# Hybrid decoder step on one core: rotary products taken from PSUM, inverse roots and gates by exp and ln on ScalarE

## The chip, the cores and the metric

One core of a Trainium2 chip runs the whole program. The metric is device microseconds (us) of one execution; three runs of the kernel before are shown. About 0.5% (16 us) is what a measurement of this kernel can tell from no change.

## What is computed

One inference step of a two-layer decoder for a prompt of 2048 tokens and 8 sample tokens, all in float32. Layer 0 is the one that the change touches:

```
u, q, k, v, gate = split_cols(h @ w_in, ...)          # h = rmsnorm(x)
q = rope(rmsnorm(q.reshape(B, L, 12, 64), qn_w), pos)
k = rope(rmsnorm(k.reshape(B, L, 12, 64), kn_w), pos)
rmsnorm(x, w) = x * rsqrt(mean(x * x) + EPS) * w
rope(x, pos)  = concat(x1 * cos - x2 * sin, x2 * cos + x1 * sin)
mixed = concat(a_out, b_out) * silu(gate)
x = x + mixed @ w_out
```

The sample tokens attend to a paged cache of 128 pages of keys and 128 of values. Layer 1 (gated DeltaNet and a spatial-gating MLP) follows with the same in- and out-projections.

## The kernel before

The program has four stages: the in-projection of layer 0 (`in_even`), prompt attention, the out-projection of layer 0 (`out_even`) and the whole of layer 1 (`odd`). Every float32 product is made of three fp32r matmuls with high and low halves (`mm3`, L167 to L169). A scheduler orders each engine's instructions when the program is built; each engine then works through its own queue in that order, and a waiting instruction holds all that stand behind it.

`in_even` treats the prompt in two halves of 1024 tokens. For each half it normalizes the tokens (`h_tile`), and then goes through a written list of jobs (`JOBS`): q, k and v in column blocks of 256, eight gate blocks, and the pooling branch. One q or k block (`qkv_block`) of 256 tokens by 256 columns is 48 matmuls into one PSUM bank (`acc`; five banks serve all the blocks and gates of this stage). Then `qk_norm_rope` runs over the block: ScalarE squares it out of the bank (`qsq`, L245), VectorE sums over 64 columns (`qss`, L247), GpSimd adds EPS and raises to the power -0.5 (`rstd`, L106 and L107), VectorE multiplies the bank by that factor (`qxn`, L250), GpSimd makes the products with the cosine and sine tables (L254 and twice L258), and VectorE adds them (`qr`, L261). The bank is free after L250. TensorE transposes `qr` (L362), ScalarE and VectorE split it into halves (`qhi`, `qlo`), and four stores to DRAM follow. There are 48 such blocks for the prompt and 6 small ones for the sample tokens.

Between the blocks, `sample_scores` walks the 128 key pages of the cache: a 384 KB load by SyncE (three buffers `kp`), a product on GpSimd or, for one page in three, on VectorE (L521), and a sum on VectorE (L522). It begins when the q blocks of the first half are issued. The weights come as units (`w_unit`): ScalarE makes the high half (`whi`), GpSimd the low half (`wlo`, L148).

A gate (`silu2_store`, L391 and L393) is one tanh on ScalarE and one multiply on VectorE out of the bank. `rstd` also serves `h_tile`, the end of each attention quad (`ss`), and layer 1.

Of the kernel before, what the change touches and what calls it, by code (L numbers as in the profile page):

```python
# [10 lines left out]
F32 = mybir.dt.float32  # L11
# [50 lines left out]
class Net:  # L62
# [28 lines left out]
    def constants(self):  # L91
        nc, I, c = self.nc, self.I, self.const
        self.ident = c.tile([P, P], F32, name="ident")
        make_identity(nc, self.ident)
        self.identb = c.tile([P, P], BF16, name="identb")
        make_identity(nc, self.identb)
        self.ones = c.tile([P, P], F32, name="ones")
        nc.gpsimd.memset(self.ones, 1.0)
        self.mhalf = c.tile([P, 1], F32, name="mhalf")
        nc.gpsimd.memset(self.mhalf, -0.5)  # L100

    def rstd(self, ms, eps=EPS):

        g = self.nc.gpsimd
        if eps:
            g.tensor_scalar(ms, ms, eps, None, ALU.add)  # L106
        g.tensor_tensor(ms, ms, self.mhalf[:ms.shape[0]].broadcast_to(list(ms.shape)), ALU.pow)  # L107
# [131 lines left out]
    def qk_norm_rope(self, pool, ps, C, S, np_, nt, ng):  # L239

        nc = self.nc
        n = nt * ng
        sq = pool.tile([P, n, 64], F32, tag="qsq", name="qsq")[:np_]
        flat = ps.rearrange("p t (g d) -> p (t g) d", d=64)
# [3 lines left out]
        self.rstd(ss)  # L248
        xn = pool.tile([P, n, 64], F32, tag="qxn", name="qxn")[:np_]
        nc.vector.tensor_tensor(xn, flat, ss[:, :, None].broadcast_to([np_, n, 64]), ALU.mult)  # L250
        a = sq
        x4 = xn.rearrange("p (t g) d -> p t g d", t=nt)
        a4 = a.rearrange("p (t g) d -> p t g d", t=nt)
        nc.gpsimd.tensor_tensor(a4, x4, C[:, :, None, :].broadcast_to([np_, nt, ng, 64]), ALU.mult)  # L254
        b = pool.tile([P, n, 64], F32, tag="qb", name="qb")[:np_]
        b4 = b.rearrange("p (t g) d -> p t g d", t=nt)
        for o in (0, 32):
            nc.gpsimd.tensor_tensor(b4[:, :, :, o:o + 32], x4[:, :, :, 32 - o:64 - o],  # L258
                                    S[:, :, None, o:o + 32].broadcast_to([np_, nt, ng, 32]), ALU.mult)
        r = pool.tile([P, n, 64], F32, tag="qr", name="qr", bufs=3)[:np_]  # L260
        nc.vector.tensor_tensor(r, a, b, ALU.add)  # L261
# [124 lines left out]
    def silu2_store(self, pool, ps, dst, r0, t0, n, ns):  # L386
# [4 lines left out]
        nc.scalar.activation(th[:, :w], ps[:, :w], AF.Tanh, scale=0.5)  # L391
        sg = th
        nc.vector.scalar_tensor_tensor(sg[:, :w], th[:, :w], 1.0, ps[:, :w], ALU.add, ALU.mult)  # L393
# [484 lines left out]
    def out_even(self):  # L878
# [18 lines left out]
        for n, t in enumerate(P3):  # L897
            t0 = t * P
# [833 lines left out]
```

## Time and profile before

| | |
|---|---|
| median of three runs | 3227.11 us (3221.92 to 3235.94) |
| the profiled execution | 3230.68 us |
| its span in the trace | 3229.0 us, 57271 instructions |
| mean granted clock of TensorE | 0.946 |
| HBM traffic | 332.41 MB read, 126.33 MB written, 142 GB/s over the span |

The span is the time between the first and the last instruction in the trace; 1.7 us of the execution lie around it. PE is TensorE, PEld its weight loads, DVE VectorE, ACT ScalarE, POOL GpSimd, SP SyncE. [...]

### The profile page before, as it was taken

What the parts mean: (1) busy time and instruction counts of PE and PEld (TensorE: products, weight loads), DVE (VectorE), ACT (ScalarE), POOL (GpSimd) and SP (SyncE); (2) the same over time, 40 slices, a digit from 0 to 9 for tenths busy, and PEclk for the clock granted to TensorE, in tenths of its full rate; (3) what the DMA queues carried; (4) which work ended last, traced back from release to release, by engine and by line L of the source; (5) the groups of instructions that cost most, each with busy time, mean ns of one, the idle gap of its engine ahead of it and who ended that gap; (6) DMA issues with size and microseconds to landing.
All of it is one profiled execution on the core that took longest, in us unless ns stands there. A gap on an engine that the chain in (4) does not pass through costs nothing. (4 is left out here: it accounts for less than half of the span.)

```text
span 3229.0 us, 57271 instructions
## 1 busy us (share of the span) xinstructions
PE 2828.4 (88%) x20425; PEld 2530.5 (78%) x20425; DVE 2221.3 (69%) x3958; ACT 1335.5 (41%) x3753; POOL 1937.4 (60%) x1532
## 2 busy tenths in 40 slices
PE   7988889997889889898988777899999988878999
PEld 7987888996777677787877667778888977767887
DVE  5565555556489989895578998667888674357652
ACT  4212121221378777773222323445555542444331
POOL 8887557996277787776576555455444335246541
PEclk9998899998999999999999889999999998979999
DMA  4455876554632444206676554435333333458542
GB/s 156 131 159 190 258 213 190 180 184 154 162 83 58 110 115 104 64 24 192 218 250 204 159 173 149 150 106 152 87 101 85 90 104 102 124 163 229 143 125 85
DMA packets 423146, 462.53 MB, mean 143 GB/s; under 512 B 84683, under 2 KB 324212, under 8 KB 422860
## 3 DMA queue, kind: packets, MB, share of 16 engines
q1 hardware_dynamic: 422860, 458.86, 47.9%
q8 instruction: 162, 2.65, 0.4%
q14 instruction: 124, 1.02, 0.1%
HBM read 332.41 MB, written 126.33 MB: 142 GB/s over the span
## 5 line engine op out<-in xcount | busy, mean ns | idle before, releaser
L167 PE MATMUL acc<-sh,whi 128*128 128x256 f32 (+2 forms) x1328 | 391.4, 295 | 12.8 <-DVE th L393 3.8
L169 PE MATMUL acc<-sh,wlo 128*128 128x256 f32 (+2 forms) x1328 | 387.3, 292 | 1.7 <-DVE wlo L148 1.3
L168 PE MATMUL acc<-sl,whi 128*128 128x256 f32 (+2 forms) x1328 | 387.8, 292 | 0.1
L167 PE MATMUL acc<-bh,whi 128*128 128x512 f32 (+2 forms) x904 | 348.6, 386 | 30.7 <-ACT raw L1183 15.0
L169 PE MATMUL acc<-bh,wlo 128*128 128x512 f32 (+2 forms) x904 | 347.9, 385 | 7.7 <-DVE wlo L148 4.2
L168 PE MATMUL acc<-bl,whi 128*128 128x512 f32 (+2 forms) x904 | 346.5, 384 | 1.8 <-DVE bl L846 1.8
L809 POOL TENSOR_TENSOR p<-p,cf 128x512 f32<-128x512 f32 (+3 forms) x240 | 239.4, 1016 | 163.7 <-ACT p L786 58.4
L786 ACT ACTIVATE p<-sc,nb 128x512 f32<-128x512 f32 (+3 forms) x480 | 300.7, 636 | 89.1 <-DVE nb L785 80.5
L599 POOL TENSOR_TENSOR kp<-kp,at 128x768 f32<-128x768 f32 x120 | 210.5, 1763 | 155.3 <-DMA kp<-in_cache_v 136.6
L785 DVE TENSOR_REDUCE nb<-sc 128x1 f32<-128x512 f32 (+3 forms) x480 | 275.8, 597 | 17.8 <-PE sc L782 8.8
L167 PE MATMUL acc<-whi,bh 128*128 128x256 f32 x864 | 253.4, 294 | 27.8 <-DVE qxn L250 24.6
L167 PEld LDWEIGHTS acc<-sh,whi 128*128 128x128 f32 (+1 forms) x1328 | 258.5, 195 | 22.9 <-ACT raw L1183 4.4
L148 POOL TENSOR_TENSOR wlo<-wraw,whi 128x1024 fp32r<-128x1024 f32 (+1 forms) x90 | 224.6, 2498 | 83.3 <-ACT whi L146 82.5
L168 PEld LDWEIGHTS acc<-sl,whi 128*128 128x128 f32 (+1 forms) x1328 | 258.9, 195 | 6.6 <-issue 2.9
L168 PE MATMUL acc<-wlo,bh 128*128 128x256 f32 x864 | 252.8, 293 | 12.0 <-POOL wlo L148 12.0
L169 PEld LDWEIGHTS acc<-sh,wlo 128*128 128x128 f32 (+1 forms) x1328 | 258.1, 194 | 5.1 <-DVE wlo L148 1.5
L169 PE MATMUL acc<-whi,bl 128*128 128x256 f32 x864 | 252.9, 294 | 0.0
L781 PE MATMUL sc<-kh,q 128*128 128x512 f32 (+2 forms) x480 | 212.4, 443 | 35.8 <-ACT p L786 34.0
L1199 DVE SCALAR_TENSOR_TENSOR cx<-raw,convw,cx 128x512 f32<-128x512 f32 x216 | 235.6, 1091 | 11.2 <-ACT cx L1197 8.7
L823 PE MATMUL pv<-v,pt 128*128 128x128 f32 x1632 | 220.1, 283 | 16.5 <-ACT pt L821 8.4
L823 PEld LDWEIGHTS pv<-v,pt 128*128 128x128 f32 x1632 | 205.9, 197 | 28.6 <-ACT pt L821 11.9
L521 POOL TENSOR_TENSOR kp<-kp,qb 128x768 f32<-128x768 f32 x88 | 170.0, 1938 | 94.9 <-DMA kp<-in_cache_k 63.9
(434 smaller groups left out, 8412.1 us busy)
## 6 DMA issues: line engine op xcount, KB each, us to landing
kp<-in_cache_k SPq DMA_DIRECT2D x128, 384.0 KB
kp<-in_cache_v SPq DMA_DIRECT2D x128, 384.0 KB
wraw<-in_w_in_e SPq DMA_DIRECT2D x56, 512.0 KB
wraw<-in_w_in_o SPq DMA_DIRECT2D x56, 512.0 KB
mc<-cat SPq DMA_DIRECT2D x72, 256.0 KB
mg<-sg SPq DMA_DIRECT2D x72, 256.0 KB
y<-cth SPq DMA_DIRECT2D x72, 256.0 KB
kh<-kh SPq DMA_DIRECT2D x48, 256.0 KB
```

What stands on the lines that cost most here:

```text
L148: e.tensor_tensor(lo, raw, hi.bitcast(F32), ALU.subtract)
L167: mm(out, ah, bh, start=first, stop=False)
L168: mm(out, ah, bl, start=False, stop=False)
L169: mm(out, al, bh, start=False, stop=last)
L521: (nc.vector if j % 3 == 2 else nc.gpsimd).tensor_tensor(k, k, qb, ALU.mult)
L599: nc.gpsimd.tensor_tensor(h3(w), h3(v), self.at[:, b, j, :, None].broadcast_to([P, NH, P]), ALU.mult)
L781: mm(sc[:, :w], qc, kh[:, c, :w], start=True, stop=False)
L785: nc.vector.tensor_reduce(nb[:, c, j:j + 1], sc[:, :n], AX.X, ALU.max, negate=True)
L786: nc.scalar.activation(p[:, c, :n], sc[:, :n], AF.Exp, bias=nb[:, c, j:j + 1], accum_out=l[:, c, j:j + 1])
L809: nc.gpsimd.tensor_tensor(p[:, 1, :n], p[:, 1, :n], cf[:, 1, j:j + 1].broadcast_to([P, n]), ALU.mult)
L823: mm(pv, tt[:, t, :], kvt[j][2][:, t, :], start=j == 0 and t == 0, stop=j * 4 + t == nk - 1)
L1199: nc.vector.scalar_tensor_tensor(x, raw[:, o + j:o + j + 512], w[:, j:j + 1], x, ALU.mult, ALU.add)
```

## The change

The rotary products are made on VectorE straight from the PSUM bank, their sum on GpSimd, and the norm's factor is applied last, by ScalarE, in eight pieces of 64 columns for each block. `rstd` becomes two ScalarE instructions, Ln and Exp, wherever `self.logs` is set and the eps is 1e-6; `self.logs` holds through layer 0 up to the eighth tile of `out_even`. The gates of layer 0 become Exp, Ln, Exp on ScalarE and a multiply on VectorE. One table set (number 6) is loaded at the start. Layer 1 keeps its instructions.

```diff
     def rstd(self, ms, eps=EPS):
+        if self.logs and eps == EPS:
+            n = ms.shape[0]
+            self.nc.scalar.activation(ms, ms, AF.Ln, bias=self.eps[:n])
+            self.nc.scalar.activation(ms, ms, AF.Exp, scale=-0.5)
+            return
...
         nc.vector.tensor_reduce(ss, sq, AX.X, ALU.add)
-        self.rstd(ss)
-        xn = pool.tile([P, n, 64], F32, tag="qxn", name="qxn")[:np_]
-        nc.vector.tensor_tensor(xn, flat, ss[:, :, None].broadcast_to([np_, n, 64]), ALU.mult)
-        a = sq
-        x4 = xn.rearrange("p (t g) d -> p t g d", t=nt)
+        a = pool.tile([P, n, 64], F32, tag="qxn", name="qxn")[:np_]
         a4 = a.rearrange("p (t g) d -> p t g d", t=nt)
-        nc.gpsimd.tensor_tensor(a4, x4, C[:, :, None, :].broadcast_to([np_, nt, ng, 64]), ALU.mult)
+        nc.vector.tensor_tensor(a4, x4, C[:, :, None, :].broadcast_to([np_, nt, ng, 64]), ALU.mult)
         b = pool.tile([P, n, 64], F32, tag="qb", name="qb")[:np_]
         b4 = b.rearrange("p (t g) d -> p t g d", t=nt)
         for o in (0, 32):
-            nc.gpsimd.tensor_tensor(b4[:, :, :, o:o + 32], x4[:, :, :, 32 - o:64 - o],
+            nc.vector.tensor_tensor(b4[:, :, :, o:o + 32], x4[:, :, :, 32 - o:64 - o],
                                     S[:, :, None, o:o + 32].broadcast_to([np_, nt, ng, 32]), ALU.mult)
+        self.rstd(ss)
         r = pool.tile([P, n, 64], F32, tag="qr", name="qr", bufs=3)[:np_]
-        nc.vector.tensor_tensor(r, a, b, ALU.add)
+        nc.gpsimd.tensor_tensor(a, a, b, ALU.add)
+        for i in range(n):
+            nc.scalar.mul(r[:, i, :], a[:, i, :], ss[:, i:i + 1])
...
-        nc.scalar.activation(th[:, :w], ps[:, :w], AF.Tanh, scale=0.5)
-        sg = th
-        nc.vector.scalar_tensor_tensor(sg[:, :w], th[:, :w], 1.0, ps[:, :w], ALU.add, ALU.mult)
+        if self.logs:
+            e = th[:, :w]
+            nc.scalar.activation(e, ps[:, :w], AF.Exp, scale=-1.0)
+            nc.scalar.activation(e, e, AF.Ln, bias=1.0)
+            nc.scalar.activation(e, e, AF.Exp, scale=-1.0, bias=self.ln2)
+            sg = th
+            nc.vector.tensor_tensor(sg[:, :w], e, ps[:, :w], ALU.mult)
...
         for n, t in enumerate(P3):
+            self.logs = n < 8
```

The scheduler lays out every queue anew. Three places matter. First, ScalarE's queue at the first k blocks of the first half; `qsq` is the square of a block, `qhi` the split of its transposed result. Before:

```order
L245 ACTIVATE qsq_1673<-acc_1611 128x512
L245 ACTIVATE qsq_1763<-acc_1701 128x512
L245 ACTIVATE qsq_1853<-acc_1791 128x512
L135 CAST qhi_1693<-tr_1688 128x512
L146 CAST whi_2012<-wraw_2014 128x1024
L146 CAST whi_2162<-wraw_2164 128x1024
L245 ACTIVATE qsq_1943<-acc_1881 128x512
```

and with the change:

```order
L263 ACTIVATE qsq_1777<-acc_1715 128x512
L118 ACTIVATE qss_1779<-qss_1779,eps_77 128x8
L119 ACTIVATE qss_1779<-qss_1779 128x8
L279 ACTIVATE qr_1788<-qxn_1781,qss_1779 128x64 x8
L263 ACTIVATE qsq_1874<-acc_1812 128x512
L118 ACTIVATE qss_1876<-qss_1876,eps_77 128x8
L119 ACTIVATE qss_1876<-qss_1876 128x8
L152 CAST qhi_1804<-tr_1799 128x512
```

The split of the first block stood behind the squares of two further blocks; it now stands behind one, and the eight multiplies of a block stand ahead of the next block's square.

Second, TensorE's queue where the same block is transposed (`tr`). Before, during the small sample matmuls that come after the fourth block on:

```order
L167 MATMUL acc_1971<-whi_1106,sh_135 8x256
L362 MATMUL tr_1688<-ident_63,qr_1685 128x128 x4
L168 MATMUL acc_1971<-wlo_1107,sh_135 8x256
L169 MATMUL acc_1971<-whi_1106,sl_136 8x256
L167 MATMUL acc_1971<-whi_1106,sh_135 8x256
```

and with the change, during the matmuls of the second block after its own:

```order
L185 MATMUL acc_1909<-wlo_1555,bh_138 128x256
L380 MATMUL tr_1799<-ident_63,qr_1788 128x128
L186 MATMUL acc_1909<-whi_1554,bl_139 128x256
L184 MATMUL acc_1909<-whi_1554,bh_138 128x256
L185 MATMUL acc_1909<-wlo_1555,bh_138 128x256
```

The transposes moved up: counted over the 48 blocks, the median number of TensorE instructions between the last matmul of a block and its first transpose goes from 196 to 79.

Third, GpSimd's queue in the second column block of q, before:

```order
L106 TENSOR_SCALAR qss_1035<-qss_1035 128x8
L148 TENSOR_TENSOR wlo_1101<-wraw_1102,whi_1100 128x1024
L107 TENSOR_TENSOR qss_1035<-qss_1035,mhalf_75 128x8
L254 TENSOR_TENSOR qsq_957<-qxn_963,rope_381 128x512
L258 TENSOR_TENSOR qb_966<-qxn_963,rope_381 128x8x32 x2
L148 TENSOR_TENSOR wlo_1107<-wraw_1108,whi_1106 128x1024
```

and with the change at the first k blocks, where the key pages begin:

```order
L548 TENSOR_TENSOR kp_1594<-kp_1594,qb_1592 128x768
L548 TENSOR_TENSOR kp_1638<-kp_1638,qb_1592 128x768
L277 TENSOR_TENSOR qxn_1781<-qxn_1781,qb_1783 128x512
L548 TENSOR_TENSOR kp_1764<-kp_1764,qb_1592 128x768
```

Five GpSimd instructions of a block (L106, L107, L254, twice L258) became one (L277), which stands among the page products (L548, L521 before).

## Rows read from the trace of the kernel before

**Rows 1.** Page, busy time of each engine over the span

```profile
PE 2828.4 (88%) x20425; PEld 2530.5 (78%) x20425; DVE 2221.3 (69%) x3958; ACT 1335.5 (41%) x3753; POOL 1937.4 (60%) x1532
```

**Rows 2.** Windows: length, busy PE, PEld, DVE, ACT, POOL, then PEclk, DMA share, GB/s

```profile
200.00:250.00 50.00, 32.31 (x235) 30.79 (x233) 32.33 (x25) 6.21 (x9) 39.97 (x30) 0.83 0.40 132
...
0.00:850.00 850.00, 743.33 (x5471) 721.61 (x5471) 470.68 (x555) 197.96 (x324) 622.39 (x493) 0.94 0.59 183
850.00:1485.00 635.00, 553.76 (x3703) 461.52 (x3703) 554.75 (x1310) 469.07 (x1500) 459.34 (x445) 0.96 0.32 82
```

**Rows 3.** Waits of TensorE, 0 to 850 us: total, times, longest

```profile
PE acc L167 <- DVE qxn L250: 26.7, 5, 14.1
PE tr L362 <- DVE qr L261: 21.5, 11, 5.8
PE acc L168 <- POOL wlo L148: 12.0, 2, 10.9
...
PE acc L488 <- DVE th L393: 9.8, 2, 6.4
```

**Rows 4.** Groups by form, 0 to 810 us: count | busy, mean ns | idle, releasers

```profile
L107 POOL TENSOR_TENSOR qss<-qss,mhalf 128x8 f32<-128x8 f32 x48 | 81.7, 1707 | 2.1
L258 POOL TENSOR_TENSOR qb<-qxn,rope 128x256 f32<-128x256 f32 x96 | 73.9, 790 | 0.0
L254 POOL TENSOR_TENSOR qsq<-qxn,rope 128x512 f32<-128x512 f32 x48 | 66.6, 1388 | 20.0 <-DVE qxn L250 19.6
...
L261 DVE TENSOR_TENSOR qr<-qsq,qb 128x512 f32<-128x512 f32 x48 | 74.8, 1559 | 64.1 <-POOL qb L258 61.5 <-PE tr L362 2.5
L521 DVE TENSOR_TENSOR kp<-kp,qb 128x768 f32<-128x768 f32 x40 | 74.3, 1857 | 92.7 <-DMA kp<-in_cache_k 88.9 <-DMA qb<-svec 3.7
L250 DVE TENSOR_TENSOR qxn<-acc,qss 128x512 f32<-128x512 f32 x48 | 32.7, 686 | 23.8 <-POOL qss L107 23.6
L247 DVE TENSOR_REDUCE qss<-qsq 128x8 f32<-128x512 f32 x48 | 32.7, 681 | 21.6 <-ACT qsq L245 21.3
```

**Rows 5.** VectorE's timeline, 202 to 236 us: start, length, instruction, idle before

```profile
202.52 8.72 DVE L521 TENSOR_TENSOR kp<-kp,qb 128x768 f32<-128x768 f32 x1
...
227.86 7.84 DVE L261 TENSOR_TENSOR qr<-qsq,qb 128x512 f32<-128x512 f32 x1 [3.56 <-POOL qb L258]
```

**Rows 6.** TensorE's timeline behind one wait, 746 to 753 us

```profile
746.38 0.55 PE L167 MATMUL acc<-whi,bh 128*128 128x256 f32 x1 [5.32 <-DVE qxn L250]
...
751.64 0.39 PE L167 MATMUL acc<-whi,bh 128*128 128x256 f32 x1
...
752.11 0.28 PE L167 MATMUL acc<-whi,bh 128*128 128x256 f32 x1
...
752.93 0.28 PE L168 MATMUL acc<-wlo,bh 128*128 128x256 f32 x1
```

**Rows 7.** Groups of ScalarE by form, and two multiplies of its timeline

```profile
L1459 ACT ACTIVATE Sd<-S,el 128x128 f32<-128x128 f32 x96 | 31.7, 394 | 14.6 <-DVE S L1477 13.8 <-DVE el L1290 0.5
...
L245 ACT ACTIVATE qsq<-acc 128x512 f32<-128x512 f32 x48 | 28.6, 597 | 164.7 <-DVE qr L261 131.6 <-PE acc L169 33.2
...
L799 ACT ACTIVATE cf<-cf 128x8 f32<-128x8 f32 x24 | 5.4, 225 | 6.0 <-DVE cf L798 5.9
...
L1024 ACT ACT_TABLE_LOAD x3 | 3.8, 1283 | 0.1
...
2071.46 0.70 ACT L1459 ACTIVATE Sd<-S,el 128x128 f32<-128x128 f32 x2
```

**Rows 8.** ScalarE's gate group, 0 to 810 us

```profile
L391 ACT ACTIVATE th<-acc 128x384 f32<-128x384 f32 (+2 forms) x39 | 17.7, 455 | 74.8 <-PE acc L169 74.8
```

**Rows 9.** Waits of all engines, 0 to 810 us, on the key pages

```profile
DVE kp L521 <- DMA kp<-in_cache_k: 88.9, 30, 7.1
...
POOL kp L521 <- DMA kp<-in_cache_k: 63.9, 28, 6.8
```

**Rows 10.** Waits of TensorE, 1485 to 2100 us, on the normalized tokens

```profile
PE h L128 <- DVE hx L123: 13.9, 7, 4.2
```

More of the change, by code (lines that the diff above doesn't have):

```diff
@@ L100, in constants, with act_set @@
         nc.gpsimd.memset(self.mhalf, -0.5)
-    def rstd(self, ms, eps=EPS):
+        self.eps = c.tile([P, 1], F32, name="eps")
+        nc.gpsimd.memset(self.eps, EPS)
+        self.ln2 = c.tile([P, 1], F32, name="ln2")
+        nc.gpsimd.memset(self.ln2, math.log(2.0))
+        self.logs = True
+        self.act_set(6)
+    def act_set(self, i):
+        nc = self.nc
+        nc.scalar.add_instruction(mybir.InstLoadActFuncSet(
+            name=nc.get_next_instruction_name(), act_func_set_id=i, ins=[], outs=[]))
+    def rstd(self, ms, eps=EPS):
+        if self.logs and eps == EPS:
[3 more added lines that the diff above has]
+            return
         g = self.nc.gpsimd
@@ L242, in qk_norm_rope @@
         n = nt * ng
+        flat = ps.rearrange("p t (g d) -> p (t g) d", d=64)
+        x4 = ps.rearrange("p t (g d) -> p t g d", d=64)
         sq = pool.tile([P, n, 64], F32, tag="qsq", name="qsq")[:np_]
-        flat = ps.rearrange("p t (g d) -> p (t g) d", d=64)
         nc.scalar.activation(sq, flat, AF.Square, scale=0.125)
@@ L390, in silu2_store @@
         th = self.t512(pool, "th")
-        nc.scalar.activation(th[:, :w], ps[:, :w], AF.Tanh, scale=0.5)
-        sg = th
-        nc.vector.scalar_tensor_tensor(sg[:, :w], th[:, :w], 1.0, ps[:, :w], ALU.add, ALU.mult)
+        if self.logs:
[5 more added lines that the diff above has]
+            nc.vector.tensor_tensor(sg[:, :w], e, ps[:, :w], ALU.mult)
+        else:
+            nc.scalar.activation(th[:, :w], ps[:, :w], AF.Tanh, scale=0.5)
+            sg = th
+            nc.vector.scalar_tensor_tensor(sg[:, :w], th[:, :w], 1.0, ps[:, :w], ALU.add, ALU.mult)
         self.store(dst[r0:r0 + P, t0:t0 + n], sg[:, :n])
```

## The prediction

> **What bounds the kernel now.** I read the page first: TensorE is busy 88% of the span and no other engine over 78% [rows 1], so time is won where TensorE waits or where its clock is low. The windows then show how the two stages that the change mostly works in stand [rows 2]. The in-projection (0 to 850 us) has TensorE busy for 743.3 of 850 us, with a granted clock of 0.94; GpSimd is the next busiest (622 us), and ScalarE has much room (198 us). Attention (635 us) has VectorE at 555 and ScalarE at 469 us. Between 200 and 250 us TensorE was busy for only 32 us and the clock was 0.83.
>
> The list of TensorE's waits gives the in-projection's 107 idle us their causes [rows 3]. The largest is 26.7 us in 5 waits on `qxn`, which frees a PSUM bank; the longest is 14.1 us. Next come 21.5 us in 11 waits of the transposes on `qr`, then 12.0 us on a weight's low half made on GpSimd, then 9.8 us on the gates. The groups show why `qxn` is late: 23.6 us of VectorE's idle time before it ended with GpSimd's power [rows 4], and VectorE's own queue was held up by a page product that took 8.72 us, where such products average 1.86 us [rows 4, 5]. The addition `qr`, a float32 sum of two SBUF tiles, also stretches: 7.84 us once and 1.56 us on average, while `qxn`, of the same size but from PSUM, keeps to 0.69 us [rows 4, 5]. Both long cases ran while GpSimd worked.
>
> **The change part by part.** All durations are from the profiled execution.
>
> *GpSimd.* The power (81.7 us), the halves' products (73.9) and the cosine products (66.6) go, 222 us for the 48 large blocks [rows 4]. The new sum is of the size of the cosine product, 1.39 us, so 48 of them cost 67 us. GpSimd loses 155 us of its 622. TensorE gains nothing from that alone; it pays only through waits.
>
> *VectorE.* `qr` and `qxn` go (107.5 us). The new product over 512 columns from PSUM should cost what `qxn` does (0.69 us). The products over 256 columns have no row; half of 0.69 and the whole of it bound them, and I take 0.40 us, because most of `qxn` is its columns. That is 48 x (0.69 + 0.80) = 72 us, or 36 us less in all. It lies beside the matmuls.
>
> *ScalarE, the norm.* Ln and Exp on 8 columns cost about 0.225 us each, as the Exp on 8 columns does [rows 7]. Eight multiplies of 64 columns have no row: 128 columns cost 0.39 us alone and 0.31 us when one follows another (0.70 less 0.39), 8 columns 0.225 us [rows 7]. I take 0.26 us, 2.1 us for eight. So each block adds 2.5 us, 122 us in all. With the gates' addition below this brings ScalarE to some 355 of 850 us. Its busy time is covered by the matmuls; its place in the queue is another matter.
>
> *Bank waits, -27 us.* A bank is now freed after the square, the sum and three products (0.60 + 0.68 + 0.69 + 0.80 = 2.8 us), with GpSimd no longer between. With five banks and some 6 us of matmuls to a block (48 at 0.117), the 26.7 us should go. If VectorE is held as long by a page product as at 202 us, half of it stays; that is the upper bound, and nothing excludes a further gain.
>
> *Slow clock behind these waits, -7 us.* [...]
>
> *Transposes, +6 us.* Here I expect a loss. A block's new path is square 0.60, sum 0.68, products 1.49, GpSimd's sum 1.39, eight multiplies 2.1: 6.3 us, and about 7 with the handoffs. The scheduler now puts the transposes a median of 79 TensorE instructions behind the block, 79 x 0.117 = 9.3 us, where it was 196, or 23 us. So 2.3 us are left. Twelve blocks run before the first key page. In the other 36, a page product waiting for its DMA stands in VectorE's or GpSimd's queue; such waits average 3.0 and 2.3 us [rows 9], and the product behind costs 1.9 us [rows 4]. If each of the 36 met one, TensorE would wait 36 x (3.0 + 1.9 - 2.3) = 94 us; if none did, the present 21.5 us would go. One block in three gives 31 us, but squares no longer wait for `qr` (131.6 us of ScalarE's idle time [rows 7]), which advances part of them; I take 28 us in place of 21.5.
>
> *Gates, +5 us.* Each has two more ScalarE instructions of about 0.455 us [rows 8] while it holds its bank; VectorE's multiply keeps its size. 39 gates by 0.91 us are 35 us of ScalarE. TensorE waits on the gates' banks twice, 9.8 us [rows 3]. If five or six gates come to be waited for, it is 5 us; bounds 0 and 35.
>
> *Out-projection, -4 us.* TensorE waits 13.9 us for normalized tokens [rows 10]. Eight of the sixteen tiles lose GpSimd's add and power and the page products ahead of them; half of their half is 4 us, bounds 0 and 14.
>
> *Attention and the rest, 0.* 24 quads swap GpSimd's power for two small ScalarE instructions, 24 x 0.45 = 11 us on an engine with 166 us free there. Attention's and layer 1's queues come out in a partly different order with nothing removed. I allow 15 us to either side, a sixth of attention's 81 idle us [rows 2].
>
> No DMA is added. SyncE's queue moves only with the scheduler: a block's stores and the `new_k_prompt` output are issued sooner against the page loads.
>
> The sum is -27 - 7 + 6 + 5 - 4 = **-27 us** against the execution's 3230.7, or 3204. That execution is 3.6 us above the median of the three runs, so against 3227.1 I predict **3200 us**.
>
> **The rivals.**
>
> *The transposes come too early (slower).* The mechanism is the one priced above at its upper end. ScalarE works in order, and the eight multiplies of a block stand ahead of the next block's square. While GpSimd holds the sum behind a page that has not arrived, ScalarE can't square the next block, nor make weights' high halves. For it: GpSimd and VectorE idle 64 and 89 us on the pages [rows 9], and the reserve fell from 16 us to 2. Against it: part of the waits fall into gates and v blocks, where nobody needs `qr`. TensorE's waits on `qr` would be 94 instead of 28: 3200 + 66 = 3266 us, or about 3280 with slow clock. It decides from an average wait of 1.1 us a block: 48 x 1.1 = 55 us eats the 27 us up. [...] Chance 0.16.
>
> *It washes out (no change).* The 27 us on the banks become waits of the transposes and gates, with the page loads setting the pace of the stage. DMA share is 0.59 there [rows 2], and the pages' waits are not touched by the change. 3227 us, chance 0.21.
>
> *Much better.* VectorE's page products fall towards the short ones, since GpSimd works 155 us less and `qr` is gone; then the transposes' 21.5, the 12.0 on the low half and the gates' waits vanish too: 27 + 7 + 21 + 12 + 10 = 77 us, 3150 us. For it: the two long VectorE instructions of rows 5. Against it: the shorter reserve. Chance 0.24.
>
> *It doesn't do what it says.* Were Ln and Exp in two table sets, every pair would load tables, 1.28 us each [rows 7]. The order of the built program has eight loads in all against seven before, so this is worth 1.3 us; chance under 0.01.
>
> **How the numbers follow.** My own case (3175 to 3211 us) has 0.38, much better 0.24, no change 0.21, slower 0.16. A difference of 0.5% is 16 us, about what a measurement of this kernel can tell from no change. So faster has 0.38 + 0.24 = 0.62, the same 0.22 (with the remaining 0.01), slower 0.16. The range runs from 3150 us (the better case's own time) to 3245 us (just past no change); a tenth of the chance lies outside at either end.
>
> **What would show it.** Right: no wait of an `acc` matmul on the bank products to speak of; waits of the transposes between 15 and 45 us, now on ScalarE's multiplies; GpSimd's busy time in the first 850 us near 465 us, ScalarE's near 355; attention beginning some 25 us sooner. Wrong: transposes' waits above 55 us; or a gain that lies in attention or layer 1, which this sum leaves at nothing; or multiplies of 64 columns above 0.31 us.

## The result and the profile after

The changed kernel takes 3143.38 us (median of 4 runs, 3142.22 to 3149.47), the kernel before 3230.73 us in the same comparison: a ratio of 0.9736 between the means of the runs (95% interval 0.9709 to 0.9763). It is faster by 87 us; 27 were forecast, and the time lies 7 us below the range's lower end.

The page of the kernel after, busy time of each engine (before: [rows 1]):

```profile
span 3142.4 us, 57680 instructions
...
PE 2812.4 (89%) x20425; PEld 2515.9 (80%) x20425; DVE 2170.1 (69%) x4012; ACT 1516.3 (48%) x4464; POOL 1688.4 (54%) x1220
```

TensorE has the same 20425 instructions. GpSimd lost 249 us and ScalarE gained 181. To see where the span lost 87 us, I cut both traces where the first score matmul of the attention starts and where its last square starts (`junk`, behind the last product with v); the same 5464 matmuls lie ahead of the first cut. Windows of before (length, busy PE, PEld, DVE, ACT, POOL, PEclk, which is the clock granted to TensorE as a share of full speed, DMA share, GB/s):

```profile
0.00:849.30 849.30, 742.63 (x5464) 721.00 (x5465) 470.64 (x554) 197.58 (x323) 622.39 (x493) 0.94 0.59 183
849.30:1481.80 632.50, 551.44 (x3696) 459.80 (x3696) 554.10 (x1309) 469.09 (x1499) 456.95 (x442) 0.96 0.31 81
```

The same windows of after, and the first 850 us:

```profile
0.00:787.80 787.80, 728.58 (x5464) 709.95 (x5465) 422.25 (x608) 367.31 (x967) 415.30 (x245) 0.97 0.63 198
787.80:1395.80 608.00, 545.51 (x3696) 450.70 (x3695) 556.77 (x1310) 473.99 (x1548) 422.69 (x396) 0.99 0.33 84
0.00:850.00 850.00, 785.52 (x5829) 754.68 (x5830) 481.42 (x770) 420.10 (x1147) 452.57 (x283) 0.97 0.61 189
```

| stage | before | after | difference | forecast |
|---|---|---|---|---|
| in-projection | 849.3 | 787.8 | -61.5 | -23 |
| attention | 632.5 | 608.0 | -24.5 | 0 |
| out-projection | 241.3 | 244.1 | +2.8 | -4 |
| layer 1 | 1505.9 | 1502.5 | -3.4 | 0 |

In the in-projection TensorE's idle time fell from 106.7 to 59.2 us (-47.5), and its busy time, at a clock of 0.97 instead of 0.94, from 742.6 to 728.6 (-14). What it still waits for there, after (total, times, longest; before: [rows 3]):

```profile
PE tr L380 <- ACT qr L279: 26.7, 8, 6.2
PE h L145 <- DVE hx L140: 10.4, 2, 10.0
PE acc L515 <- DVE th L416: 8.7, 1, 8.7
PE acc L504 <- DVE th L416: 4.8, 1, 4.8
PE h L145 <- DVE bl L153: 3.6, 5, 1.2
...
PE side L567 <- DVE mp L564: 1.2, 1, 1.2
PE acc L185 <- POOL wlo L165: 0.5, 1, 0.5
```

The row on the bank products is gone altogether. The weight's low half fell from 12.0 to 0.5 us, and the end of the sample scores, which cost 9.4 us before (first of these two rows; the second is the start of the half), to 1.2. In the waits of before:

```profile
PE side L540 <- DVE mp L537: 9.4, 1, 9.4
PE h L128 <- DVE bl L136: 6.9, 2, 6.0
```

The prices of the new instructions, groups by form of after, 0 to 780 us (count | busy, mean ns | idle before, releasers):

```profile
L279 ACT ACTIVATE qr<-qxn,qss 128x64 f32<-128x64 f32 x384 | 96.9, 335 | 48.7 <-POOL qxn L277 48.4
...
L548 DVE TENSOR_TENSOR kp<-kp,qb 128x768 f32<-128x768 f32 x40 | 65.7, 1643 | 94.3 <-DMA kp<-in_cache_k 94.2
L277 POOL TENSOR_TENSOR qxn<-qxn,qb 128x512 f32<-128x512 f32 x48 | 65.6, 1367 | 82.5 <-DVE qb L273 74.2 <-ACT qss L119 5.3 <-DVE sl L153 3.0
...
L273 DVE TENSOR_TENSOR qb<-acc,rope 128x256 f32<-128x256 f32 x96 | 35.8, 413 | 0.0
...
L414 ACT ACTIVATE th<-th,ln 128x384 f32<-128x384 f32 x31 | 19.1, 615 | 0.8
```

The prices agree with the forecast (0.41 us for the product over 256 columns against 0.40). A multiply of 64 columns shows a mean of 0.335 us, but eight in a row take 2.02 us, as the timeline further down has it, so each starts 0.25 us after the last.

### The profile page after: what moved, and what is told of

The parts are those of the page before. It is cut to its first block, busy times and chain, and to the rows that moved or that the text cites. A ratio compares the mean times of both kernels' runs of the same rounds, so it can differ in the third digit from the quotient of the medians.

```text
span 3142.4 us, 57680 instructions
## 1 busy us (share of the span) xinstructions
PE 2812.4 (89%) x20425; PEld 2515.9 (80%) x20425; DVE 2170.1 (69%) x4012; ACT 1516.3 (48%) x4464; POOL 1688.4 (54%) x1220
## 5 line engine op out<-in xcount | busy, mean ns | idle before, releaser
L813 ACT ACTIVATE p<-sc,nb 128x512 f32<-128x512 f32 (+3 forms) x480 | 302.3, 642 | 74.0 <-DVE nb L812 63.1
L812 DVE TENSOR_REDUCE nb<-sc 128x1 f32<-128x512 f32 (+3 forms) x480 | 276.0, 598 | 17.5 <-PE sc L809 9.1
L184 PEld LDWEIGHTS acc<-sh,whi 128*128 128x128 f32 (+1 forms) x1328 | 260.3, 196 | 17.5 <-ACT raw L1211 6.0
L548 POOL TENSOR_TENSOR kp<-kp,qb 128x768 f32<-128x768 f32 x88 | 168.9, 1925 | 183.6 <-DMA kp<-in_cache_k 133.8
```

What stands on the lines that cost most here:

```text
L184: mm(out, ah, bh, start=first, stop=False)
L548: (nc.vector if j % 3 == 2 else nc.gpsimd).tensor_tensor(k, k, qb, ALU.mult)
L812: nc.vector.tensor_reduce(nb[:, c, j:j + 1], sc[:, :n], AX.X, ALU.max, negate=True)
L813: nc.scalar.activation(p[:, c, :n], sc[:, :n], AF.Exp, bias=nb[:, c, j:j + 1], accum_out=l[:, c, j:j + 1])
```

## The experiments

Theory: the gain of the in-projection comes from taking GpSimd out of the way that frees a bank; what is left are the transposes, which follow their block too closely. Rivals: GpSimd's smaller load; one half of the change alone; the new roots and gates. The table has the start of the attention, its length, the median of the runs, and the ratio to before with its interval. The ratios are to before as it was measured beside each kernel (medians of 3228.2 to 3230.7 us). Stage times come from one trace each, of an execution that in bank_root was 7 us above its median and in fill_pages4 9 us below. What follows the attention takes 1745 to 1764 us in these traces. after, attn_pow, fill_attn and attn_path have the same instructions in the in-projection and start the attention at 781.6 to 787.8: a stage moves by 6 us without an edit to it, and differences of that size are not given to an edit here.

| kernel | start | attention | median | ratio |
|---|---|---|---|---|
| before | 849.3 | 632.5 | 3230.7 | |
| after | 787.8 | 608.0 | 3143.4 | 0.9736 (0.9709 to 0.9763) |
| rope_only | 773.0 | 625.0 | 3154.1 | 0.9767 (0.9751 to 0.9783) |
| logs_only | 791.9 | 608.7 | 3148.6 | 0.9755 (0.9735 to 0.9774) |
| attn_pow | 782.7 | 621.3 | 3166.7 | 0.9790 (0.9767 to 0.9812) |
| factor_dve | 790.8 | 606.2 | 3145.9 | 0.9738 (0.9722 to 0.9754) |
| best_mix | 776.1 | 612.8 | 3138.6 | 0.9726 (0.9700 to 0.9752) |
| fill_even | 764.8 | 612.4 | 3131.9 | 0.9696 (0.9668 to 0.9724) |
| fill_attn | 781.6 | 606.5 | 3147.9 | 0.9750 (0.9721 to 0.9778) |
| gate_tanh | 819.2 | 656.1 | 3227.3 | 1.0003 (0.9985 to 1.0021) |
| bank_root | 824.0 | 622.8 | 3200.4 | 0.9917 (0.9889 to 0.9945) |
| wait96 | 782.1 | 609.9 | 3141.7 | 0.9739 (0.9721 to 0.9756) |
| mix96 | 785.2 | 614.5 | 3150.0 | 0.9754 (0.9731 to 0.9776) |
| attn_path | 784.7 | 616.5 | 3152.4 | 0.9763 (0.9743 to 0.9783) |
| one_page | 752.9 | 611.9 | 3115.8 | 0.9638 (0.9609 to 0.9668) |
| pages4 | 774.6 | 613.7 | 3140.9 | 0.9717 (0.9686 to 0.9748) |
| raw3 | 783.7 | 615.6 | 3147.9 | 0.9739 (0.9709 to 0.9768) |
| fill_pages4 | 757.0 | 616.2 | 3135.2 | 0.9712 (0.9686 to 0.9738) |

### Each half alone

**rope_only** keeps the rotary products from PSUM with the factor last; roots are GpSimd's power again and gates tanh, everywhere.

```diff
-        self.logs = True
-        self.act_set(6)
+        self.logs = False
...
-            self.logs = n < 8
```

> The rotary part alone; roots by GpSimd's power and gates by tanh as before. My theory (the bank no longer waits for the root, GpSimd loses its products): attention begins some 45 us sooner than before (near 805 us), attention itself lasts as before (about 633 us), total 3185 us. Rival (the roots on ScalarE carry the gain, since a block's path still crosses GpSimd's power): attention begins near 840 us, total 3220 us.

**logs_only** keeps ScalarE's roots and gates, with `qk_norm_rope` as before (bank times root on VectorE, products on GpSimd, sum on VectorE).

```diff
+        self.rstd(ss)
+        nc.vector.tensor_tensor(xn, flat, ss[:, :, None].broadcast_to([np_, n, 64]), ALU.mult)
-        nc.vector.tensor_tensor(a4, x4, C[:, :, None, :].broadcast_to([np_, nt, ng, 64]), ALU.mult)
+        nc.gpsimd.tensor_tensor(a4, x4, C[:, :, None, :].broadcast_to([np_, nt, ng, 64]), ALU.mult)
...
-        nc.gpsimd.tensor_tensor(a, a, b, ALU.add)
-        for i in range(n):
-            nc.scalar.mul(r[:, i, :], a[:, i, :], ss[:, i:i + 1])
+        nc.vector.tensor_tensor(r, a, b, ALU.add)
```

> Roots and gates by exp and ln alone; rotary part as before. My theory: the bank waits for qxn shrink but stay (the products still stand on GpSimd), attention begins 15 us sooner (near 834 us); attention, which here has the same queue order as with the whole change, lasts about 608 us as with the whole change; total 3190 us. Rival (roots carry the in-projection's gain too): attention begins near 795 us, total 3150 us.

Either half alone gives most of it: rope_only starts the attention 76 us earlier than before, logs_only 57, and both together 62. They do not add up, which fits that each takes GpSimd's power out of the step that frees the bank. Both expectations missed: rope_only's start came 32 us sooner than expected, and logs_only landed on the numbers of its rival (795 and 3150), so the roots carry much of the in-projection's gain as well when they come alone. Roots and gates on ScalarE, added to the rotary part, make the in-projection 15 us longer (773.0 to 787.8).

### Load of GpSimd, or its place

**fill_even** gives GpSimd's load back, off the way: a power and two products on a scratch tile behind each block's sum (1.65 + 0.61 + 0.61 us).

```diff
-        nc.gpsimd.tensor_tensor(a, a, b, ALU.add)
+        add = nc.gpsimd.tensor_tensor(a, a, b, ALU.add).ins
+            with self.tc.issue_after(add):
+                nc.gpsimd.tensor_tensor(f[:, :8], f[:, :8], self.mhalf.broadcast_to([P, 8]), ALU.pow)
+                nc.gpsimd.tensor_tensor(f, f, f, ALU.mult)
+                nc.gpsimd.tensor_tensor(f, f, f, ALU.mult)
```

> The whole change, and behind the sum of each large block GpSimd does a power over 8 columns and two products over 256 columns on a scratch tile that nobody reads: 3.1 us a block, about what the change took from it (3.3 us). If GpSimd's load made the in-projection slow: attention begins near 835 us, total 3190 us. If it was the path of a bank through GpSimd's queue (my theory, since either half of the change alone takes GpSimd out of that path): attention begins within 15 us of 788 us, total 3145 to 3160 us.

**bank_root** is the cell across: the load stays away, but the root by GpSimd's power stands again ahead of the step that frees the bank. The rotary products on VectorE then read the scaled tile `xn` in SBUF, where rope_only's read the bank. Against rope_only:

```diff
+        self.rstd(ss)
+        xn = pool.tile([P, n, 64], F32, tag="qxn", name="qxn")[:np_]
+        nc.vector.tensor_tensor(xn, flat, ss[:, :, None].broadcast_to([np_, n, 64]), ALU.mult)
+        x4 = xn.rearrange("p (t g) d -> p t g d", t=nt)
...
-        for i in range(n):
-            nc.scalar.mul(r[:, i, :], a[:, i, :], ss[:, i:i + 1])
```

> The root of the in-projection goes back to GpSimd's power and back into the way that frees a bank (bank times root first), while the rotary products stay on VectorE, so that GpSimd's work of 9.2 us a block stays away. Theory 'it is GpSimd in the bank's way, not GpSimd's load': the bank products wait on the scaled tile again, 15 to 27 us, and the attention starts at 800 to 830 us, 25 us or more behind rope_only's 773. Rival 'it is GpSimd's load': no such wait over 5 us and a start at 770 to 790. The gates use tanh and the power is in the attention too, so the attention should take 620 to 632 us; the whole 3165 to 3200 by the theory, near 3155 by the rival.

Windows of the in-projection, fill_even:

```profile
0.00:764.80 764.80, 727.50 (x5465) 708.95 (x5466) 415.56 (x608) 366.70 (x967) 558.63 (x390) 0.97 0.64 204
```

and bank_root:

```profile
0.00:824.00 824.00, 741.46 (x5464) 718.51 (x5465) 505.89 (x662) 197.55 (x323) 542.30 (x387) 0.96 0.60 189
```

Waits of TensorE in bank_root, 0 to 785 us:

```profile
PE tr L380 <- POOL qr L279: 21.8, 9, 6.0
...
PE acc L183 <- DVE qxn L268: 9.8, 5, 4.9
```

GpSimd is about equally busy in the two (559 and 542 us), and the stage differs by 59 us. rope_only has 534 us there and starts at 773. So the load, up to fill_even's 559 of before's 622 us, is not the cause. For the place speaks that the stage takes 849.3 and 824.0 us in the two kernels with GpSimd's power ahead of the bank's release, and 765 to 792 in the kernels that have it elsewhere or on ScalarE without table loads (one_page and the fourth page buffer left aside). The wait on `qxn` came back with 9.8 us only, below the 15 that were expected, but the stage lost 51 us to rope_only. How much of the 51 is the detour was not separated, since VectorE has 87 us more to do in bank_root. 33 of them are the multiplication by the root; most of the others come from the rotary products, which take longer from SBUF:

```profile
L276 DVE TENSOR_TENSOR qb<-qxn,rope 128x256 f32<-128x256 f32 x96 | 67.2, 740 | 0.0
...
L272 DVE TENSOR_TENSOR qsq<-qxn,rope 128x512 f32<-128x512 f32 x48 | 53.7, 1119 | 1.1
```

From the bank the same products take 0.41 and 0.68 us in rope_only, as in after. That the products read the bank is thus a rival to the detour for a part of the 51 us, and no run tests it alone.

That fill_even is faster than after (its four runs, 3129.9 to 3133.7, lie all below the four of after) was not foreseen. Its queues come out in another order, and TensorE waits 10.4 us on `qr` in place of 26.7. The traces show what goes with it: how long GpSimd stands at key pages that have not arrived, in after and then in fill_even.

```profile
POOL kp L548 <- DMA kp<-in_cache_k: 133.8, 47, 21.5
```

```profile
POOL kp L556 <- DMA kp<-in_cache_k: 76.0, 31, 20.2
```

In the kernel before it was 63.9 [rows 9]. A GpSimd with less to do gets to the next page sooner and waits longer there, and a block's sum may stand behind that page. Take the kernels that apply the factor last and read all pages (without gate_tanh and its table loads). In the five with more work for GpSimd in the in-projection (rope_only, best_mix, mix96, fill_even, fill_pages4) GpSimd waits 71 to 83 us for pages and TensorE 10 to 18 us on `qr`; in the eight others it is 116 to 138 and 20 to 27 us. This is read from the traces behind the runs, not tested by one.

### One table set

**gate_tanh** is the change with layer 0's gates by tanh, beside Ln and Exp for the roots.

```diff
         th = self.t512(pool, "th")
-        if self.logs:
+        if False:
```

> The whole change, but the gates by tanh as before, which is not in the table set that Ln and Exp share: 162 table loads in the program in place of 8, 154 x 1.28 = 198 us of ScalarE. My theory (ScalarE's reserve doesn't cover them, because the loads stand in the path of each block's root and its transposes): 3200 us or more. Rival (covered by ScalarE's idle time): 3145 us.

The groups of table loads in gate_tanh; L118 is the Ln of a root, L119 its Exp, L813 the Exp of the attention's scores, L418 the gates' tanh:

```profile
L118 ACT ACT_TABLE_LOAD x77 | 98.8, 1283 | 1.4
...
L119 ACT ACT_TABLE_LOAD x60 | 77.0, 1283 | 1.1
...
L813 ACT ACT_TABLE_LOAD x16 | 20.5, 1283 | 0.3
...
L418 ACT ACT_TABLE_LOAD x2 | 2.6, 1283 | 0.0
```

With seven more that makes 162 loads instead of 8, some 200 us of ScalarE, and the whole gain is gone (3227.3 us). My theory held in its number and in the wait (the transposes wait 45.3 us), but not in its account of the loads. Only two of them stand before a tanh. 153 are Ln and Exp taking turns, 77 and 76, and 48 of these lie in the attention, where no gate runs. By these counts the first tanh puts out table set 6, which was loaded by name at the start; from then on, wherever Ln and Exp follow each other, each loads a set (1.28 us). So the 84 us are the price of losing set 6, and not of tanh gates as such. What they would cost beside such roots with set 6 loaded by name again behind them was not run.

**best_mix** has tanh gates and GpSimd's power throughout the in-projection, one table load behind the last tanh, and ScalarE's roots from there through the attention.

```diff
-        self.logs = True
-        self.act_set(6)
+        self.logs = False
...
+            for t in self.tanhs:
+                es.enter_context(self.tc.issue_after(t))
+            self.tabload = self.act_set(6)
...
-                    self.rstd(ss)
+                    self.logs = True
+                    with self.tc.issue_after(self.tabload):
+                        self.rstd(ss)
+                    self.logs = False
```

> The rotary part as changed, roots and gates of the in-projection by power and tanh, and one table load before attention so that only attention's 24 roots go by Ln and Exp. My theory (the two gains lie in different stages: the rotary part gives the in-projection's, attention's roots give attention's; in the in-projection Ln and Exp only add ScalarE work and waits): attention begins near 773 us as in the rotary part alone and lasts 608 us as in the whole change, total 3130 us, some 13 us below the whole change. Rival (the second part needs the first to be on ScalarE throughout, or the table load disturbs): 3143 us or more.

It comes near the shorter stage of each (776.1 for 773.0, 612.8 for 608.0) and takes 3138.6 us, 9 more than expected; its interval overlaps that of after. Its trace has 9 table loads: with set 6 loaded by name behind the last tanh, the attention's Ln and Exp need no other.

### Which engine applies the factor

**factor_dve** makes the last step one multiply of 512 columns on VectorE, to see whether a shorter path shortens the transposes' wait.

```diff
-        for i in range(n):
-            nc.scalar.mul(r[:, i, :], a[:, i, :], ss[:, i:i + 1])
+        nc.vector.tensor_tensor(r, a, ss[:, :, None].broadcast_to([np_, n, 64]), ALU.mult)
```

> The whole change, but the norm's factor is applied by one VectorE multiply of 512 columns in place of eight ScalarE pieces of 64. [...] Rival (a VectorE product of two SBUF tiles is held up while GpSimd works, as qr was at 1.56 us, and VectorE's queue holds page products): no gain, waits of the transposes stay or grow, total 3145 to 3165 us.

3145.9 against 3143.4 us, no difference, as the rival had it. TensorE waits 26.1 us on this `qr` where it waited 26.7 on ScalarE's, so the eight multiplies are not what delays the transposes. The one multiply, of two SBUF tiles, took 1.10 us on average, where `qxn`, out of the bank, took 0.69 [rows 4]; against the 2.02 us of eight in a row the path is 0.9 us shorter.

### What delays the transposes

**wait96** asks that the transposes of a block come at least 96 TensorE instructions (two blocks) behind its last matmul, by program order and by `issue_after`; counted in the queue, the median goes from 79 to 105 and the least from 64 to 97. **mix96** is the same on best_mix (108 to 130).

```diff
+        while self.tails and self.nmm - self.tails[0][0] >= lag:
+            f = self.tails.pop(0)[1]
+            with self.tc.issue_after(self.lastmm):
+                f()
```

> The change as it is, but the transposes of a block are put at least two blocks (96 TensorE multiplies) behind its last multiply, by program order and a wish of order; measured in the queue the median distance is 105 instead of 79 and the least 97 instead of 64. Theory 'the transposes wait because the scheduler leaves them too short a reserve': their wait falls from 26.7 us to under 13, the attention starts at 765 to 778 us instead of 787.8, the attention stays at 604 to 612 us, and the whole is 3120 to 3136. Rival 'the wait is set by ScalarE's eight multiplies and would only move on': the wait appears at another place (the banks, the key pages), start at 783 or later and the whole 3140 to 3150.

> The same wish of order on best_mix (tanh gates and GpSimd's power in the in-projection, roots by logarithm on ScalarE in the attention); median distance 130 instead of 108, least 97 instead of 70. Theory of the reserve: the transposes' wait falls from 12.7 us to under 6, start of the attention at 766 to 772 instead of 776.1, the whole 3124 to 3134. Rival: nothing left to gain there, 3136 to 3142.

Waits of TensorE on `qr` in wait96 and (second fence) in mix96:

```profile
PE tr L397 <- ACT qr L281: 19.9, 10, 6.8
```

```profile
PE tr L398 <- ACT qr L282: 17.5, 8, 5.0
```

My theory fell. 26 more instructions of reserve in the one take 7 us off the wait, 22 more in the other add 5 (12.7 in best_mix). The whole time is the same in wait96; mix96's median is 11 us above best_mix's, with intervals that overlap. So I looked at the longest wait in after. TensorE's timeline, then ScalarE's, VectorE's and GpSimd's ahead of it:

```profile
701.72 0.47 PE L380 MATMUL tr<-ident,qr 128*128 128x128 f32 x1 [6.20 <-ACT qr L279]
```

```profile
685.64 0.60 ACT L263 ACTIVATE qsq<-acc 128x512 f32<-128x512 f32 x1 [2.57 <-PE acc L186]
...
696.36 1.04 ACT L163 CAST whi<-wraw 128x1024 fp32r<-128x1024 f32 x1 [9.08 <-DMA wraw<-in_w_in_e]
697.31 0.30 ACT L118 ACTIVATE qss<-qss,eps 128x8 f32<-128x8 f32 x1
...
701.08 2.02 ACT L279 ACTIVATE qr<-qxn,qss 128x64 f32<-128x64 f32 x8 [2.74 <-POOL qxn L277]
```

```profile
691.75 0.95 DVE L549 TENSOR_REDUCE sc<-kp 128x12 f32<-128x768 f32 x1 [4.88 <-POOL kp L548]
692.62 0.68 DVE L265 TENSOR_REDUCE qss<-qsq 128x8 f32<-128x512 f32 x1
```

```profile
689.87 1.85 POOL L548 TENSOR_TENSOR kp<-kp,qb 128x768 f32<-128x768 f32 x1 [8.07 <-DMA kp<-in_cache_k]
...
697.48 2.34 POOL L165 TENSOR_TENSOR wlo<-wraw,whi 128x1024 fp32r<-128x1024 f32 x1 [3.29 <-ACT whi L163]
699.78 1.26 POOL L277 TENSOR_TENSOR qxn<-qxn,qb 128x512 f32<-128x512 f32 x1
```

From the square (685.6) to the last multiply (703.1) this block took 17.5 us, where its own instructions need 6.3. VectorE's sum stood behind a reduction that waited for a page product on GpSimd, which waited 8.1 us for its page's DMA; ScalarE's root stood behind a weight's cast that waited 9.1 us for its DMA; GpSimd's sum stood behind that weight's low half. None of the block's own inputs was late: the queues run in order, and what stood ahead was. Four kernels part the pages from the weights.

**one_page** loads one key page once, and every product reads it; the other 127 pages are not read, so its scores are not the program's. **pages4** has a fourth buffer for pages in the in-projection, **raw3** a third one for raw weights, **fill_pages4** is fill_even with the fourth page buffer.

```diff
-                k = self.page(pool, I["cache_k"], b, j)
-                (nc.vector if j % 3 == 2 else nc.gpsimd).tensor_tensor(k, k, qb, ALU.mult)
+                k = pool.tile([P, 768], F32, tag="kp", name="kp", bufs=3)
+                (nc.vector if j % 3 == 2 else nc.gpsimd).tensor_tensor(k, page, qb, ALU.mult)
```

```diff
-                k = self.page(pool, I["cache_k"], b, j)
+                k = self.page(pool, I["cache_k"], b, j, 4)
```

```diff
-W0 = 4, 4, 2
+W0 = 4, 4, 3
```

> The change, with the first layer's key pages not read: one page is loaded once and every multiply takes it (reading the other pages is left out). Theory 'late key pages, standing ahead of the block's steps in the in-order queues, make the transposes wait': the waits of the transposes fall from 26.7 us to under 10, the attention starts at 750 to 770 us instead of 787.8. Rival 'late weights or the distance in the queue': 20 us or more stay, start at 780 or later. The rest of the program should take what it takes in the change (2354 us from the start of the attention on), so 3104 to 3124 by the theory, 3134 or more by the rival.

> The change, with four buffers of key pages in the in-projection instead of three. Theory of the late key pages: the waits of the transposes fall to 10 to 20 us, the attention starts at 768 to 782, the whole 3122 to 3137. Rival: no difference from the change, start 785 to 790, the whole 3139 to 3148.

> The change, with three buffers of raw weights in the in-projection instead of two. By the theory of the late key pages hardly a difference: start of the attention 782 to 790, the whole 3136 to 3146. Rival 'the late weights that ScalarE's queue waits for (57 us of idle time before the cast, 10 times) make the transposes wait': their waits fall under 15 us, the start comes at 765 to 778, the whole 3120 to 3134.

> fill_even (3131.9 us, transposes' waits 10.4 us) with four buffers of key pages. Theory of the late key pages: most of the gain is already there, start of the attention 757 to 765 instead of 764.8, the whole 3122 to 3132. Rival: no difference or, by another order of the queues, a loss: 3130 to 3145.

Waits on `qr`, one_page, then raw3:

```profile
PE tr L380 <- ACT qr L279: 8.3, 4, 6.2
```

```profile
PE tr L380 <- ACT qr L279: 26.9, 9, 7.0
```

ScalarE's waits for raw weights, in after and then in raw3:

```profile
ACT whi L163 <- DMA wraw<-in_w_in_e: 57.0, 10, 17.7
```

```profile
ACT whi L163 <- DMA wraw<-in_w_in_e: 6.1, 5, 3.7
```

raw3 takes ScalarE's wait for weights away, and the transposes wait as before (26.9). Without the pages' transfers they wait 8.3 us, and the stage ends 35 us sooner. So the pages are the largest part of what keeps them, with the reservation that one_page also lowers the DMA share of the stage (0.44 for 0.63) and with it whatever else waits for transfers: ScalarE's wait for weights is 6.8 us there. And fill_even reads all pages and waits 10.4 us, so late pages need not cost TensorE much; the order that they meet does. A fourth buffer helps the stage (774.6) and TensorE's wait hardly (23.1, where 10 to 20 was expected); the medians of pages4 and fill_pages4 can't be told from those of the kernels they come from.

### The attention

**attn_pow** puts GpSimd's power back in the attention alone, **fill_attn** keeps ScalarE's root there and adds the same power on scratch numbers behind GpSimd's multiply, and **attn_path** puts it between root and multiply.

```diff
+                    self.logs = False
                     self.rstd(ss)
+                    self.logs = True
```

```diff
-                    nc.gpsimd.tensor_tensor(ob, ob, ss[:, :, None].broadcast_to([P, 4, P]), ALU.mult)
+                    m = nc.gpsimd.tensor_tensor(ob, ob, ss[:, :, None].broadcast_to([P, 4, P]), ALU.mult).ins
+                    with self.tc.issue_after(m):
+                        nc.gpsimd.tensor_tensor(self.fill, self.fill, self.mhalf.broadcast_to([P, 4]), ALU.pow)
```

```diff
                     self.rstd(ss)
+                    nc.gpsimd.tensor_tensor(ss, ss, self.one1.broadcast_to([P, 4]), ALU.pow)
                     nc.gpsimd.tensor_tensor(ob, ob, ss[:, :, None].broadcast_to([P, 4, P]), ALU.mult)
```

> The whole change, but attention's 24 roots back on GpSimd's power. My theory (attention's 24 us come from those roots, by GpSimd's time or by the order that the scheduler makes of it): attention begins near 788 us and lasts about 630 us, total 3167 us. Rival (attention is faster because of what it inherits from an earlier, less loaded start): it lasts about 610 us, total 3145 us.

> The whole change, and behind the last GpSimd product of each attention quad a power over 4 columns on a scratch tile that nobody reads, 1.04 us, so that GpSimd has most of its former load in attention. If that load made attention slower (its waits on GpSimd's p product, 12 to 15 us with the power and 5 us without): attention lasts about 620 us, total 3157 us. Rival (the root's own way from the last tile of a quad to its product, or the order that goes with it): attention lasts about 608 us, total 3143 us. The scheduler's order for attention is a third one here, so a result between the two is open.

> The change, but in the attention ScalarE's root is followed by one more power on GpSimd (exponent 1) on the same four numbers, so that GpSimd's 1.6 us stand again in the way from the sum of squares to the scaled output; the load on GpSimd is that of fill_attn, whose attention took 606.5 us with the same power off the way. Theory 'the roots' gain in the attention is their shorter way to the output': 618 to 630 us for the attention and 3155 to 3168 in all. Rival 'it is the order of the queues that the scheduler makes': the attention can come out anywhere; below 612 us the way is not what counts. VectorE's order in the attention is a fourth one, unlike the change's and unlike before's.

Windows of the attention, fill_attn and then attn_path:

```profile
781.60:1388.10 606.50, 539.74 (x3696) 450.19 (x3695) 553.75 (x1309) 474.92 (x1547) 448.88 (x419) 0.99 0.32 84
```

```profile
784.70:1401.20 616.50, 547.22 (x3696) 455.27 (x3695) 554.72 (x1310) 474.82 (x1548) 448.32 (x419) 0.98 0.32 83
```

All four kernels with GpSimd's power for the attention's roots take 621 to 633 us; the twelve with ScalarE's root alone and no further table loads take 606 to 616. So 5 us at least and 14 between the means go with the root there, and GpSimd's load is not why (fill_attn, 606.5). attn_pow's 3166.7 us agree with the 3167 expected partly by luck: its attention was 9 us shorter than expected, and what follows it 17 us longer than in after. attn_path, with the same load as fill_attn, is 10 us longer, below what the theory of the way asked for (618 to 630) and at the edge of the other group. VectorE's order differs from kernel to kernel, and its part can't be separated from the way's; this stays open.

TensorE's own waits in the attention, before and then after, speak against the plain form of that theory:

```profile
PE sc L781 <- ACT p L786: 34.0, 40, 5.4
PE tr L819 <- POOL p L815: 14.4, 12, 5.5
```

```profile
PE sc L808 <- ACT p L813: 20.9, 39, 4.0
...
PE tr L846 <- POOL p L842: 4.6, 7, 1.2
```

On a quad's scaled output (`ob`) it waited 1.8 us before and 0.5 after. What fell are its waits for the exponentials, which free the score banks, and for GpSimd's products on `p`.

## Why the prediction was wrong

The sum was 60 us short. Of these 24 lie in waits of the in-projection that it put at nothing, 24.5 in the attention that it put at nothing too, and 7 in the clock.

- **Bank waits, -27: right.** The row is gone.
- **Slow clock, -7: too small.** TensorE's busy time fell by 14 us. No run shows the term by itself; it was my estimate for the stretches behind three waits of one kind (5.2, 14.1 and 5.3 us). Behind the last of these, in before, 24 matmuls started 0.219 us apart at a granted clock of 0.50, and from 752.11 us on they came 0.117 us apart at 1.00 [rows 6]: 2.4 us more for the 24, and 7 if all three stretches were alike. The low half's and the scores' waits went as well, and the clock of the stage rose from 0.94 to 0.97. How much of it belongs to which wait was not measured.
- **Transposes, +6: right in size, by luck in part.** 26.7 us against 28. Pages ahead of a block's steps were in the term, and one_page bears them out. But it set each page's delay against the reserve, by which wait96's three more microseconds (26 times 0.117) would have ended nearly all of the wait; 19.9 us stayed. The delays are fewer and longer than it had them, 8 waits of up to 6.2 us where it reckoned with 12 of 2.6; in the longest, late pages and a late weight met in three queues. And it took the pages' waits from before, where GpSimd's were 63.9 us; with less to do GpSimd waited 133.8.
- **Gates, +5: too large.** TensorE's waits on `th` went from 16.1 (9.8 and 6.3 on smaller rows) to 15.0; in rope_only, which has the tanh, they are 12.6. The prices per instruction were near (0.49 to 0.62 us for 0.455), and the matmuls covered most of them. rope_only shows a price elsewhere: roots and gates together lengthen the stage by 15 us, most of it in waits of the transposes (12.0 there, 26.7 here).
- **The term that was missing: other waits in the in-projection, counted as nothing.** The low half (-11.5), the end of the scores (-8.2) and the starts of the halves (-4) make 24 us. I had the low half and the gates in the rival "much better" only, under the condition that VectorE's page products become short; they became only a little shorter (1.86 to 1.64 us) [rows 4], and the waits went all the same. This is the step that failed in this stage: the sum let the detour over GpSimd cost TensorE only what stood under the bank's own name, and put the waits that the diff doesn't name at nothing, where they gave 24 us. bank_root brings 9.8 us back under that name and 51 us in all, with VectorE's longer products in them. Which queue freed the low half and the scores' end was not settled: rope_only still waits 7.5 us on the low half with 534 us of work on GpSimd, and fill_even, with 559, waits 1.9.
- **Attention, 0: the other step that failed, -24.5.** I priced 24 swaps by ScalarE's 11 us of work, on an engine with room, and gave nothing for what leaves GpSimd's queue there, an addition and a power of 1.4 us together for each quad, nor for a new order of the queues. attn_pow puts 13 us on the roots; the other 11 (632.5 to 621.3) stay with the other order of the queues, and rope_only has 7.5 of them without any change in the attention. Why the roots are worth 13 stays open.
- **What would show it.** GpSimd's busy time in the first 850 us was to be 465 us and is 453, ScalarE's 355 and is 420, of which 53 lie behind the start of the attention. The waits of the transposes lie in the band named (15 to 45), the attention starts 61.5 instead of 25 us sooner, and a gain in the attention was named as the sign that the sum is wrong. The third sign, multiplies of 64 columns above 0.31 us, can be read either way: their mean is 0.335, and in a row they follow each other by 0.25.
- **Out-projection, -4: not seen** (+2.8; between after and attn_pow, with the same instructions behind the attention, what follows it differs by 17). The wait on normalized tokens is still there (14.5 us for 13.9) [rows 10].

The slower rival had its mechanism half right: pages that have not arrived do hold a block up through the order of the queues, but TensorE waits 26.7 us and not 94, in 8 waits for 48 blocks. The factor in one VectorE instruction changes nothing here: factor_dve takes 3145.9 us for 3143.4. The 0.69 us of `qxn` [rows 4] are the price of a product out of the bank; from two SBUF tiles it was 1.10. The rival "no change" held that the pages' waits are not touched by the change; they went from 152.8 to 228.1 us on VectorE and GpSimd together, and TensorE gained all the same. The rival "much better" (3150) came nearest, by partly other ways. The case that Ln and Exp lie in two table sets did not happen; in gate_tanh Ln and Exp load sets in turn (77 and 76 loads), at 84 us in all.

## What to carry to other kernels

Ask of an engine in the way to a buffer's release not how busy it is but what else stands in its queue: fill_even and bank_root have GpSimd about equally busy (559 and 542 us) and differ by 59 us in one stage, though VectorE's work differs too. Ask also what an engine that gets free will wait for next (GpSimd waited 133.8 us for key pages in after, 63.9 in before). A stall that names a producer may belong to something ahead of that producer; follow each queue back until a DMA or a busy engine is reached, before distance or instruction count is blamed. Count the table loads by the instruction that they stand before, since the one that started them may be another (153 of gate_tanh's 162 stand before an Ln or an Exp, two before a tanh). And list every wait of the stage in the sum, also those that the diff does not touch, with what frees them.

## What the runs showed of the hardware beyond that

One VectorE instruction that reads two SBUF tiles lasted longer than any GpSimd instruction beside it. VectorE's timeline of after, a product over 16 columns:

```profile
212.77 5.25 DVE L490 TENSOR_TENSOR d<-us,icnt 128x16 f32<-128x16 f32 x1
```

and GpSimd's beside it:

```profile
211.95 2.42 POOL L165 TENSOR_TENSOR wlo<-wraw,whi 128x1024 fp32r<-128x1024 f32 x1
214.32 1.31 POOL L277 TENSOR_TENSOR qxn<-qxn,qb 128x512 f32<-128x512 f32 x1
215.57 2.41 POOL L165 TENSOR_TENSOR wlo<-wraw,whi 128x1024 fp32r<-128x1024 f32 x1
217.94 0.73 POOL L277 TENSOR_TENSOR qxn<-qxn,qb 8x256 f32<-8x256 f32 x1
```

The other instruction of that form took 0.17 us. This one ended at 218.0, when the third of four GpSimd instructions in an unbroken row did; only the first of the three (211.95 to 214.37) was running when it started. The products of the change, with one operand in PSUM, keep to 0.41 and 0.68 us on average, also beside GpSimd (0.68 at 201.94, with a sum on GpSimd from 202.18 to 203.47); bank_root's, from SBUF, take 0.74 and 1.12. No run here varied this alone.
